# The down projection of an encoder trunk: 18 of 22 f-tiles by seven products, each product over all output pairs in turn

## The chip, the cores and the metric

The kernel runs on one core of one Trainium2 chip. The metric is the device time of one execution in microseconds (us), lower is better. The kernel before takes 1707.04 us, the median of 3 runs (1706.98 to 1707.08). Engines are named as in the profile: PE is TensorE (its matmuls), PEld its weight loads, DVE is VectorE, ACT is ScalarE, POOL is GpSimd, SP is SyncE, which here only issues DMAs.

## The reference, cut to what matters

One layer of a bidirectional encoder trunk: a convolution mixer and a gated linear recurrence side by side, a merge, and a gated feed-forward network (FFN) with a final norm. D_MODEL = 1024, SEQ = 1024, D_FF = 2816. Only the FFN bears on the change:

```python
def _conv_glu_ffn(h, w_up, dw_w, dw_b, w_down):
    up = jnp.einsum("bsd,df->bsf", h, w_up)
    gate, val = jnp.split(up, 2, axis=-1)
    gate = _dwconv_centred(gate, dw_w, dw_b)
    return jnp.einsum("bsf,fd->bsd", jax.nn.silu(gate) * val, w_down)
...
    x = x + _conv_glu_ffn(h2, ffn_w_up[layer], ...)
    return _rmsnorm(x, final_norm_w)
```

## The kernel before

Activations lie with the feature on the 128 partitions and the position along the free axis, in two halves of 512 positions. D_FF is 22 f-tiles of 128, D_MODEL is 8 output tiles of 128. Every float32 product is made of three matmuls on parts: a matrix is split into a high part (rounded by a cast on ACT) and a low part (the difference, on DVE, line 125, helper `split`), and `mm3` (lines 149 to 151) adds high-high, high-low and low-high in one PSUM bank. So each weight page and each activation page costs one ACT cast and one DVE subtraction before PE can use it, and the third matmul needs the low part of the weights.

The up projection (`ffn_job`, `pair_job`) makes two f-tiles' worth of work as a 2x2 block product by seven products in place of eight (Strassen's scheme as Winograd arranged it): P1, P2, P6, P7, P5, P4, P3 in that order, with sums of blocks on both sides. After each f-tile, `gated` makes silu(conv(gate)) * value, half by half: ACT L1708, two DVE operations L1710, ACT Silu L1718, DVE L1719 and L1720, and stores the half in the DRAM scratch `d_g`. For f-tiles that go into the seven-product part of the down projection, `g_sums` also makes the four sums of a pair of f-tiles and stores them in `d_gc`.

The down projection before has three parts. `std_down` takes the first 6 f-tiles plainly (8 output tiles x 2 halves x 6 f-tiles x 3 matmuls = 288 matmuls) and copies the results into the 16 result pages `xr`. `seven_down` takes the next 12 f-tiles in 2 rounds of 6, by seven products: a pair job for each of 4 pairs of output tiles (i, i+4), 3 k-steps a product (2 x 4 x 7 x 3 x 3 = 504 matmuls). Its results are added to `xr` on DVE (`take`, L1883; `f`, L1887), and in the last round POOL adds the residual `d_x2` to each page by an accumulating DMA (L1890). The sums of weight blocks that products 7, 5, 6 and 3 need are made by DVE adds inside the pair job, or for three of the eight jobs ahead of time (`down_sums`, L2036 to L2044), through the DRAM scratch `d_ws`. `last_jobs` takes the last 4 f-tiles plainly, adds them to `xr` (`final_evac`, L1954), and turns, normalises and stores the output.

What sets the order: PE's order is written out by hand (generators driven by `run_jobs` and `Stream`; `later(n, ...)` runs a chore n pieces of PE work later). The order of the other engines is made by a list scheduler, but instructions given to `pin` (`split(..., late=True)`, and the ACT steps of `gated`) keep their order in the program among themselves. Each engine, and SP's queue, then works strictly in its order. `std_job` splits its weights without `late`, the pair jobs with it. In SP's queue a DMA also waits for the landing of the one eight before it, as eight semaphores go round.

Page pools that matter: weight pages `wp` 4 (high and low of two items), `wr` 2 raw pages, activation pages `hx` 32 and `gx` 16, landing pages `ev` 3 and `tm` 4.

## Time and profile before

| | before |
|---|---|
| median of 3 runs | 1707.04 us |
| the profiled execution's own time | 1706.98 us |
| its span | 1705.0 us |
| mean granted PE clock | 0.999 |
| PE busy, share of the span | 99% |
| DVE, ACT busy | 74%, 49% |
| DMA, mean | 180 GB/s |

The span begins with the first and ends with the last instruction; 2.0 us of the execution lie around it. Busy PE is not PE at its peak, since matmuls overlap: what counts is the step from one matmul's start to the next one's. A matmul that starts late shows as idle time before it with what released it.

### The profile page before, as it was taken

Reading aid. Unit: us, or ns where it says so; the run is one execution under the profiler, and the core shown is the slowest. Engines: PE = TensorE matmul, PEld = TensorE weight load, DVE = VectorE, ACT = ScalarE, POOL = GpSimd, SP = SyncE. Lnnn points to the kernel's source line nnn. Section 1 sums busy time; section 2 is a strip of 40 time slices with the busy share of each in tenths; the row PEclk is TensorE's granted clock in tenths of the full one; section 3 lists DMA queues with packets and bytes.
Section 4 is the critical chain, followed back from the end, with each engine's and each line's share of the span. In section 5 each row is a group of like instructions: output and inputs, shape, how many; then the busy total and the mean of one; then the engine's idle time right before and its main releaser. Section 6 shows DMA issues by size and latency. Waiting matters only on the chain.

```text
span 1705.0 us, 30406 instructions
## 1 busy us (share of the span) xinstructions
PE 1688.6 (99%) x11719; PEld 1408.2 (83%) x11719; DVE 1269.3 (74%) x1938; ACT 827.3 (49%) x1562; POOL 245.9 (14%) x287
## 2 busy tenths in 40 slices
PE   9999999999999999999999999999999999999998
PEld 6788888888888888888888888888888888888787
DVE  5889899887678888888565467676777776657865
ACT  7454343335476777776432345444344434442334
POOL 1312222200001111111100003122222222000110
PEclk9999999999999999999999999999999999999999
DMA  7887887866573444436797455686777776773842
GB/s 240 284 213 186 191 196 172 205 187 206 165 236 100 139 129 134 129 116 221 241 294 243 128 167 176 153 171 143 172 164 178 164 183 149 237 260 102 212 98 99
DMA packets 332871, 306.17 MB, mean 180 GB/s; under 512 B 17454, under 2 KB 244918, under 8 KB 332726
## 3 DMA queue, kind: packets, MB, share of 16 engines
q1 hardware_dynamic: 285366, 265.42, 48.8%
q0 software_dynamic: 47360, 38.81, 15.4%
q8 instruction: 92, 1.51, 0.4%
q14 instruction: 53, 0.43, 0.1%
HBM read 201.40 MB, written 84.93 MB: 168 GB/s over the span
## 4 chain that ended last, share of the span: by engine, by line
PE 70%; ACT 1%; DVE 1%; DMA 0%; issue 0%; POOL 0%; POOLq 0%; ACTq 0%; DVEq 0%
PE mm L149 16%; PE mm L151 16%; PE mm L150 16%; PE sc L149 3%; PE sc L150 3%; PE sc L151 3%; PE ob L1433 2%; PE tr L149 2%; PE tr L150 2%; PE tr L151 2%; PE sc L1247 1%; PE sc L1333 1%; PE mm L1392 1%; PE sc L1392 1%; PE ob L1247 1%; PE tr L1382 0%
## 5 line engine op out<-in xcount | busy, mean ns | idle before, releaser
L149 PE MATMUL mm<-hx,wp 128*128 128x512 f32 x1068 | 425.7, 399 | 0.0
L151 PE MATMUL mm<-hx,wp 128*128 128x512 f32 x1068 | 417.0, 390 | 0.5 <-DVE wp L125 0.5
L150 PE MATMUL mm<-hx,wp 128*128 128x512 f32 x1068 | 416.2, 390 | 0.6 <-POOL hx L125 0.6
L125 ACT CAST wp<-wr 128x1024 fp32r<-128x1024 f32 (+2 forms) x146 | 146.9, 1006 | 224.3 <-PE mm L150 165.0
L151 PEld LDWEIGHTS mm<-hx,wp 128*128 128x128 f32 x1068 | 200.5, 188 | 44.6 <-DVE wp L125 1.6
L149 PEld LDWEIGHTS mm<-hx,wp 128*128 128x128 f32 x1068 | 200.6, 188 | 40.6 <-ACT wp L125 0.2
L150 PEld LDWEIGHTS mm<-hx,wp 128*128 128x128 f32 x1068 | 200.8, 188 | 39.9 <-POOL hx L125 1.0
L125 DVE TENSOR_TENSOR wp<-wr,wp 128x1024 fp32r<-128x1024 f32 (+2 forms) x144 | 169.5, 1177 | 39.8 <-ACT wp L125 39.4
L1065 DVE SCALAR_TENSOR_TENSOR acc<-gl,v_b,acc 128x1024 f32<-128x1024 f32 x120 | 153.5, 1280 | 1.7
L441 ACT COPY su<-mm 128x512 f32<-128x512 f32 x82 | 47.8, 583 | 84.4 <-PE mm L151 84.3
L1371 POOL DMA_DIRECT2D S<-D x64 | 36.1, 571 | 281.1 <-ACT jk L1438 125.3
L125 ACT CAST wq<-sw 128x1024 fp32r<-128x1024 f32 x41 | 43.2, 1054 | 61.3 <-PE mm L150 32.9
L1194 DVE TENSOR_TENSOR qF<-qF,tb 128x512 f32<-128x512 f32 x96 | 65.9, 686 | 9.5 <-ACT A L1228 8.9
L149 PE MATMUL tr<-hx,wp 128*128 128x512 f32 x180 | 70.1, 390 | 0.0
L151 PE MATMUL tr<-hx,wp 128*128 128x512 f32 x180 | 70.1, 389 | 0.0
L150 PE MATMUL tr<-hx,wp 128*128 128x512 f32 x180 | 70.0, 389 | 0.0
L1194 DVE TENSOR_TENSOR kG<-kG,tb 128x512 f32<-128x512 f32 x96 | 65.9, 687 | 4.0 <-ACT A L1228 2.2
L1710 DVE SCALAR_TENSOR_TENSOR tm<-gp,v_a,tm 128x512 f32<-128x512 f32 x88 | 66.0, 750 | 3.3 <-ACT tm L1708 1.3
L302 POOL DMA_DIRECT2D sw<-in_ffn_w_up_dram x38 | 49.8, 1502 | 116.0 <-DMA sw<-in_ffn_w_up_dram 72.4
L149 PE MATMUL sc<-hy,wq 128*128 128x512 f32 x164 | 63.9, 390 | 0.0
L151 PE MATMUL mm<-hy,wp 128*128 128x512 f32 x164 | 63.8, 389 | 0.0
L149 PE MATMUL mm<-hy,wp 128*128 128x512 f32 x164 | 63.8, 389 | 0.0
(377 smaller groups left out, 3721.9 us busy)
## 6 DMA issues: line engine op xcount, KB each, us to landing
wr<-in_w_in_dram SPq DMA_DIRECT2D x48, 512.0 KB, 5.6
wr<-in_ffn_w_up_dram SPq DMA_DIRECT2D x22, 512.0 KB, 5.6
sw<-in_w_in_dram SPq DMA_DIRECT2D x38, 256.0 KB, 3.1
d_g<-ft SPq DMA_DIRECT2D x38, 256.0 KB, 2.0
sw<-in_ffn_w_up_dram SPq DMA_DIRECT2D x38, 256.0 KB, 3.2
sw<-in_ffn_w_up_dram POOLq DMA_DIRECT2D x38, 256.0 KB, 6.7
wr<-sw POOLq DMA_DIRECT2D x32, 256.0 KB, 3.2
wr<-wr POOLq DMA_DIRECT2D x32, 256.0 KB, 3.3
```

What stands on the lines that cost most here:

```text
L125: parts = A.copy(hi, src), eng.tensor_tensor(lo, src, hi.bitcast(F32), op=ALU.subtract)
L149: T.matmul(acc, whi[:, k, :], ahi, start=first, stop=False, skip_group_check=again)
L150: T.matmul(acc, whi[:, k, :], alo, start=False, stop=False, skip_group_check=again)
L151: T.matmul(acc, wlo[:, k, :], ahi, start=False, stop=last, skip_group_check=again)
L302: G.dma_start(o, a, accum_op=ALU.add)
L441: A.copy(t, acc)
L1065: V.scalar_tensor_tensor(acc, g[:, k : k + S], tap(k), acc, op0=ALU.mult, op1=ALU.add)
L1194: return V.tensor_tensor(o, a, b, op=op)
L1247: T.matmul(b[g, o], A_t[:, at : at + 32], Q_t(at), start=True, stop=True)
L1371: G.dma_start(S_t[g : g + 32, :, g : g + 32], D_t[g : g + 32])
L1392: T.matmul(u[:, sl], kTs[d][:, sl], v[:, c, :], start=True, stop=True)
L1710: V.scalar_tensor_tensor(c, g[:, o + k : o + k + H], vec("fdw", k * NF + j), c, op0=ALU.mult, op1=ALU.add,)
```

## The change

The plain first part and the two rounds go. In their place 18 f-tiles (0 to 17) form one block product: even f-tiles are the upper half, odd ones the lower, 9 k-steps a product. The loop is turned round: a product is made for all four pairs of output tiles before the next product comes, so that its 9 activation pages are used four times. There are 28 items (product i, pair p) of 27 matmuls, in the order P1, P2, P6 for p = 0..3, then P7 and P4 for each p, then P5, P3 for p = 0..3. In all 756 matmuls stand in place of 792.

- Weights: an item loads 8 k-steps as one raw page of 128x1024; the ninth k-step of all four pairs is one page of 128x512 (`load_ninth`). Weight splits are made with `late`, so they are pinned.
- Sums of weight blocks now all go through `d_ws`: 36 tasks-worth of (p, k), each 4 loads of 64 KB, three in-place DVE adds (now pinned) and one store. 18 of them run during the up projection on `ev` pages, one an up job; the other 18 run early in the down projection as 10 tasks, in two `ws` pages of two k-steps.
- `g_sums` and its stores to `d_gc` run for nine pairs of f-tiles in place of six.
- PSUM: P1, P6, P5, P3 of a pair accumulate in one bank over the whole stage (`rows[p]`, four banks), P2, then P7 and P4 in `cols[p]`. P4 adds onto P7 in the same bank, after ACT has copied P7 out.
- Results: ACT copies P2, P7, P7+P4 and the last row into `xr`; DVE adds or subtracts the row bank for P2, P4 and P5 (12 operations where there were 56); the 16 accumulating DMAs of `d_x2` are spread over the stage.

The diff, cut:

```diff
-    FIRST, NS, SEVENS = 6, 3, 2
-    LAST0 = FIRST + 2 * NS * SEVENS
+    NS, LAST0 = 9, 18
+    d_ws = [dp.tile([P, 4, NS * P], F32, name=f"d_ws_{n}") for n in range(ND // 2)]
...
-            if hf and FIRST <= j < LAST0:
+            if hf and j < LAST0:
...
+    def down_sums(p, ks, page_of):
+        n = ks.stop - ks.start
+        t = page_of(n)
+        for q, (row, i) in enumerate(((0, p), (0, p + NK2), (1, p + NK2), (1, p))):
+            nc.sync.dma_start(t[:, q], down_rows(row, i)[:, ks])
+        def add():
+            for o, a in ((slice(0, 2), slice(1, 3)), (slice(2, 3), slice(0, 1)), (slice(3, 4), slice(2, 3))):
+                pin(V.tensor_tensor(t[:, o], t[:, o], t[:, a], op=ALU.add))
+            nc.sync.dma_start(d_ws[p]..., t)
+        later(DOWN_LATE, add)
...
-    for half in range(2):
-        for f in range(FIRST):
-            later(4, load_g(f, half))
-            s_ffn.fill(1)
+    for k in range(NS):
+        later(4, load_operand(1, k))
+        s_ffn.fill(1)
+    later(4, load_ninth(1))
     s_ffn.drain()
     advance_chores(1 << 10)
...
+    def down_job(g):
+        i, p = items[g]
+        def prep():
+            if g == 0:
+                for n in range(3):
+                    load_raw(n)
...
+            w = split(*pages, raws.pop(g), V, True)
+            load_raw(g + 3)
+            return w
+        def run(w):
+            if i == 1:
+                rows[p] = bank("mm" if p < 3 else "sc")
+            elif i in (2, 7):
+                cols[p] = bank(next(col_banks))
+            acc = cols[p] if i in (2, 7, 4) else rows[p]
+            fresh = i in (1, 2, 7)
+            for k in range(NS):
...
+            o, half = p + NK2 * (i in (4, 7, 5)), int(i in (7, 5, 3))
+            t = xr[o][half]
+            if i in (2, 4, 7, 3):
+                A.copy(t, acc)
+            if i in (2, 4, 5):
+                V.tensor_tensor(t, t, rows[p], op=ALU.add if i == 2 else ALU.subtract)
+            if i in (2, 4, 5, 3):
+                added(t, o, half)
...
+    for n, (p, ks) in enumerate(tasks):
+        later(3 + 2 * n, lambda p=p, ks=ks: down_sums(p, ks, down_page))
```

How the order moves, at three places. In the changed kernel's own numbering, lines 1654, 1656, 1664, 1665, 1666 and 1687 are the former 1708, 1710, 1718, 1719, 1720 and 1741; 126 is the former 125.

First, ACT where the up projection ends and the down projection begins. `gp` is the last f-tile's gate. Before, the rows at the end of `gated`, and the casts of weights for the first plain jobs (`wp_15359` is that of the first job):

```order
L1708 ACTIVATE tm_15152<-gp_12008,v_c,v_a 128x512
L125 CAST wp_15359<-wr_15357 128x768
L1718 ACTIVATE tm_15152<-tm_15152 128x512
...
L125 CAST wp_15377<-wr_15375 128x768
L125 CAST hx_15301<-tm_15257 128x512
L125 CAST hx_15307<-tm_15271 128x512
L1708 ACTIVATE tm_15311<-gp_12009,v_c,v_a 128x512
L1718 ACTIVATE tm_15311<-tm_15311 128x512
L1708 ACTIVATE tm_15319<-gp_12009,v_c,v_a 128x512
L125 CAST wp_15434<-wr_15432 128x768
L1718 ACTIVATE tm_15319<-tm_15319 128x512
```

Now, the same place (`wp_15543` is the high part of item 0's weights, `wp_15607` that of item 2):

```order
L126 CAST hx_15477<-ev_15432 128x512
L1654 ACTIVATE tm_15489<-gp_12010,v_c,v_a 128x512
L1664 ACTIVATE tm_15489<-tm_15489 128x512
L1654 ACTIVATE tm_15497<-gp_12010,v_c,v_a 128x512
L1664 ACTIVATE tm_15497<-tm_15497 128x512
L126 CAST wp_15543<-wr_15537 128x1024
L126 CAST wp_15549<-wr_15539 128x1024
L126 CAST hx_15589<-tm_15535 128x512
L126 CAST hx_15601<-tm_15562 128x512
L126 CAST wp_15607<-wr_15541 128x1024
```

The first weights of the down projection stood one f-tile ahead of the last gating; they now stand behind all of it, and the same holds on DVE for the low part.

Second, DVE some 24 us into the changed down projection, where nothing like it stood before. `ws` are the pages of the stored sums, `wq_15747` and `wq_15820` the low parts of the weights of items 4 and 5 (P2, pairs 0 and 1), `gx_15814` that of the ninth weight page of P2:

```order
L1784 TENSOR_TENSOR ws_15649<-ws_15649 128x512
L1784 TENSOR_TENSOR ws_15649<-ws_15649 128x256 x2
L126 TENSOR_TENSOR wq_15747<-sr_15553,wq_15746 128x1024
L126 TENSOR_TENSOR gx_15760<-tm_15701,gx_15759 128x512
L1784 TENSOR_TENSOR ws_15682<-ws_15682 128x256
L1784 TENSOR_TENSOR ws_15682<-ws_15682 128x128 x2
L126 TENSOR_TENSOR gx_15790<-tm_15732,gx_15789 128x512
L1784 TENSOR_TENSOR ws_15709<-ws_15709 128x512
L1784 TENSOR_TENSOR ws_15709<-ws_15709 128x256 x2
L126 TENSOR_TENSOR gx_15814<-tm_15763,gx_15813 128x512
L126 TENSOR_TENSOR wq_15820<-sr_15611,wq_15819 128x1024
```

The adds of the fourth, fifth and sixth task of stored sums stand ahead of splits that PE waits for.

Third, DVE where item 8 (P6, pair 0) begins. `xr_15516` is the result page of item 7, `wq_15994` and `wq_16052` the weights of items 8 and 9, `ws_15832` the tenth and last task, `gx_15921` to `hx_16030` the activation pages of P6 from its fourth on, `hx_16045` its ninth weight page:

```order
L126 TENSOR_TENSOR wq_15994<-sr_15823,wq_15993 128x1024
L1924 TENSOR_TENSOR xr_15516<-xr_15516,sc_15752 128x512
L1784 TENSOR_TENSOR ws_15832<-ws_15832 128x256
L126 TENSOR_TENSOR wq_16052<-sr_15889,wq_16051 128x1024
L1784 TENSOR_TENSOR ws_15832<-ws_15832 128x128 x2
L126 TENSOR_TENSOR gx_15921<-ev_15873,gx_15920 128x512
...
L126 TENSOR_TENSOR hx_16030<-ev_15985,hx_16029 128x512
L126 TENSOR_TENSOR hx_16045<-ev_16010,hx_16044 128x512
```

Six of the nine pages that P6 reads are split only behind the evacuation of the item before it and behind the last sums.

## The prediction

> **What bounds the kernel now.** I read the head of the page and the busy time, the list of what PE waited for, PE's timeline at the start of the down projection, and then the busy time of stretches.

> ```profile
> span 1705.0 us, 30406 instructions
> PE 1688.6 (99%) x11719; PEld 1408.2 (83%) x11719; DVE 1269.3 (74%) x1938; ACT 827.3 (49%) x1562; POOL 245.9 (14%) x287
> PE sc L149 <- ACT su L441: 0.6, 1, 0.6
> PE mm L151 <- DVE wp L125: 0.5, 1, 0.5
> ```

> PE is busy throughout, and its waits are few and short. So a removed matmul is worth one step of PE, and any new wait of PE is lost in full. The timeline's columns are start, duration, engine, line, what is written and read:

> ```profile
> 1463.47 0.39 PE L151 MATMUL mm<-hy,wp 128*128 128x512 f32 x1
> 1463.69 0.39 PE L149 MATMUL mm<-hx,wp 128*128 128x512 f32 x1
> ...
> 1464.15 0.39 PE L151 MATMUL mm<-hx,wp 128*128 128x512 f32 x1
> ...
> 1465.96 0.39 PE L150 MATMUL mm<-hx,wp 128*128 128x512 f32 x1
> ...
> 1644.65 0.39 PE L149 MATMUL mm<-hx,hx 128*128 128x512 f32 x1
> ```

> The first row is the last matmul of the up projection, the second the first of the down projection, with no gap. From 1463.69 to 1465.96 there are ten steps: 2.27 / 10 = 0.227 us a step, although one matmul shows 0.39. The first matmul of `last_jobs` starts at 1644.65, so the part that is rewritten takes 1644.65 - 1463.69 = 180.96 us for its 792 matmuls.

> The profiled execution took 1706.98 us (span 1705.0 and 2.0 around it), 0.06 below the median of 1707.04. All sums below are made against 1706.98.

> **What the change removes: 9.4 us.** 756 matmuls at 0.227 take 171.6 us if none waits: 180.96 - 171.6 = 9.4. Of this 36 x 0.227 = 8.2 are the removed matmuls, and the other 1.2 are short gaps of before, which go with the loops that had them:

> ```profile
> 1590.00:1600.00 10.00, 9.21 (x40) 7.02 (x39) 9.74 (x17) 2.00 (x4) 1.73 (x2) 1.00 0.89 258
> ```

> (window, length, then busy us of PE, PEld, DVE, ACT, POOL, granted clock, DMA share, GB/s). PE stood still for 0.8 us here beside a nearly full DVE. DVE also loses 44 of 56 evacuations, but DVE isn't what sets the end.

> **What it adds, first: the handover, 9.6 us.** The order of ACT shows item 0's weight cast behind the second Silu of the last f-tile, and DVE's order its low part behind the last L1720. PE has nothing else to do. Before, the same chain ran under running matmuls:

> ```profile
> 1464.22 0.68 DVE L1741 TENSOR_TENSOR gp<-mm,rs 128x512 f32<-128x512 f32 x1
> 1464.82 0.95 DVE L125 TENSOR_TENSOR wp<-wr,wp 128x768 fp32r<-128x768 f32 x1
> 1465.68 1.29 DVE L125 TENSOR_TENSOR hx<-tm,hx 128x512 fp32r<-128x512 f32 x2
> 1466.89 1.53 DVE L1710 SCALAR_TENSOR_TENSOR tm<-gp,v_a,tm 128x512 f32<-128x512 f32 x2
> 1469.12 0.69 DVE L1719 TENSOR_TENSOR tm<-tm,rs 128x512 f32<-128x512 f32 x1 [0.70 <-ACT tm L1718]
> 1469.85 0.69 DVE L1720 TENSOR_TENSOR ft<-ft,tm 128x512 f32<-128x512 f32 x1
> 1470.46 1.53 DVE L1710 SCALAR_TENSOR_TENSOR tm<-gp,v_a,tm 128x512 f32<-128x512 f32 x2
> 1468.45 0.63 ACT L1718 ACTIVATE tm<-tm 128x512 f32<-128x512 f32 x1 [2.13 <-DVE tm L1710]
> L125 ACT CAST wp<-wr 128x1024 fp32r<-128x1024 f32 x127 | 133.4, 1050 | 204.4 <-PE mm L150 146.3 <-PE tr L150 32.8 <-DMA wr<-wr 15.5
> L125 DVE TENSOR_TENSOR wp<-wr,wp 128x1024 fp32r<-128x1024 f32 x127 | 155.7, 1226 | 24.9 <-ACT wp L125 24.6
> ```

> On the clock of before: `gp` starts at 1464.22, 0.60 to the next; one split of 0.6 in place of the three shown: the first L1710 pair starts at 1465.4. From there 2.23 to L1719 (1466.89 to 1469.12), 0.73 to L1720, 0.61 to the second pair: 1469.0. Its Silu starts 1.56 after it (1466.89 to 1468.45) and takes 0.63: 1471.2. The cast takes 1.05: PE may start at 1472.2. DVE is free at 1469.0 + 2.23 + 0.73 + 0.69 = 1472.6, and the low part takes 1.23: the third matmul starts at 1473.8, where 1464.15 was undisturbed. That is 9.65 us; 9 to 10.5 with a queue's delay. This term alone eats the gain.

> **Second: the stored sums beside the first items, 12 us.** An item lasts 27 x 0.227 = 6.13 us. DVE now adds ten tasks, in its fixed order between splits that PE needs, and they pass through two pages:

> ```profile
> L2042 DVE TENSOR_TENSOR sr<-sr,sr x6: 551/558/560, 1484.1 to 1497.8; 128x384 f32<-128x384 f32 x6
> DMA to landing us min/median/max: 3.9/5.6/7.4
> tm<-d_g SPq DMA_DIRECT2D x21, 256.0 KB, 3.5
> d_g<-ft SPq DMA_DIRECT2D x4, 256.0 KB, 2.0
> 1486.79 0.39 SPq L2036 DMA_DIRECT2D sr<-in_ffn_w_down_dram  x1
> ```

> A page's round trip: four issues of about 0.4 (1.6), landing about 3.5 behind the last (2.5 to 5, between the rows of 256 KB and 384 KB), adds 1.4, store about 3 (2 to 4; 256 KB take 2.0 when little else runs): 9.5 us for two tasks, before any queueing on DVE or SP. Counting from the start of item 0: the low part of item 3 waits for a `wp` page, that is for PE at about 11.4; the second task's adds, behind it, end at 15.0. The fourth's then end a round trip later, at 24.6, and item 4's low part, behind them, at 25.8; PE needs it at 24.75: a wait of 1.05. The sixth's end another round trip and 1.9 of adds and splits ahead of them later, at 36.0, and the ninth page of P2, behind them, is split at 36.7, where PE needs it at 31.2 (24.5, the 1.05 and 24 steps of the item): 5.5. Item 5 behind that costs about 0.5. At item 8 the evacuation of item 7, the last adds and the next low part (1.23) stand ahead of P6's fourth page: 2.0; and P6's ninth page, which needs the last store, a load and a split: 2.8. Together about 12; with the short landings 6, with the long ones 18. I take 12, since the landing is the row nearest in size.

> **Third: P4 onto P7, 3.2 us.** P4 starts in the bank that ACT must first copy:

> ```profile
> L441 ACT COPY su<-mm 128x512 f32<-128x512 f32 x82 | 47.8, 583 | 84.4 <-PE mm L151 84.3
> ```

> PE has no other work between P7 and P4 of a pair. The last matmul ends 0.39 - 0.227 = 0.16 after its step, the copy takes 0.58: about 0.8 with the signal, four times. The wait of 0.6 quoted at the start is of this kind, so 2.4 to 4.

> **Fourth: the entry to the last jobs, 2.4 us.** Their first weight casts now stand on ACT behind the copy of the last row bank, which waits for the last matmul:

> ```profile
> 1648.49 0.62 ACT L125 CAST gx<-wr 128x512 fp32r<-128x512 f32 x1 [12.76 <-DMA wr<-in_ffn_w_down_dram]
> ```

> 0.16 + copy 0.58 + two casts of 0.62, and part of a low part (0.69): 2.4, between 1.5 and 3.

> **Fifth: the clock, 2.7 us.** PE has never stood still for long in the trace of before, except at its end:

> ```profile
> 1697.22 0.41 PE L1970 MATMUL sc<-ident,xr 128*128 128x128 f32 x2 [0.39 <-DVE xr L1954]
> 1698.00:1700.00 2.00, 0.00 (x0) 0.00 (x0) 1.02 (x5) 0.68 (x5) 0.70 (x1) 1.00 0.00 0
> 1700.00:1702.00 2.00, 0.00 (x0) 0.00 (x0) 0.68 (x2) 0.79 (x2) 0.00 (x0) 0.54 0.45 186
> ```

> The granted clock is still 1.00 two us behind the last matmul and 0.54 after 1700. Waits of 8 us and 5.5 us are longer than that, so PE comes back at about half clock. How fast it recovers the trace can't show. Between at once (0) and 3 us lost each, I take as long at half clock as it took to fall, 2.7 us: 1.35 lost, twice.

> [...]

> **Added, at nothing: the up projection.** 18 early tasks and three more pairs of `g_sums` add about 1 us of DVE adds to a job, 256 KB of loads and a store.

> ```profile
> 1250.00:1300.00 50.00, 50.00 (x222) 41.44 (x221) 37.91 (x52) 19.80 (x28) 11.34 (x10) 1.00 0.83 191
> ```

> PE is full while DVE has 12 of 50 us free and DMA a sixth. PE's work hides it: 0, and 2 at most if it comes late.

> **Sum.** -9.4 + 9.6 + 12 + 3.2 + 2.4 + 2.7 = +20.5: 1706.98 + 20.5 = 1727. Low ends: -9.4 + 9 + 6 + 2.4 + 1.5 + 0 = +9.5, 1716.5. High ends: -9.4 + 10.5 + 18 + 4 + 3 + 6 + 2 = +34, 1741.

> **The rivals.** *The stored sums hide.* If loads and stores land at their shortest and DVE gets to each add at once, the second term falls to 0 to 4 and the clock's to half: +7 to +11 less a little at the other ends, 1710 to 1717. For it: DVE is busy only 11.4 of 20 us at this place before.

> ```profile
> 1463.00:1483.00 20.00, 20.00 (x90) 16.56 (x89) 11.40 (x17) 8.26 (x14) 0.00 (x0) 1.00 0.80 242
> ```

> Against: a fixed order with two pages, and a round trip of over 9 us.

> *DMA is the bound.* The first 65 us move about 18 x 512 KB of sums, 10 weight pages of 512 KB and 18 or more pages of 256 KB, some 20 MB or 308 GB/s, an estimate.

> ```profile
> 1490.00:1500.00 10.00, 10.00 (x46) 8.29 (x45) 7.79 (x14) 3.47 (x6) 0.00 (x0) 1.00 1.05 345
> ```

> 345 GB/s was had only at full share. If landings double to 7 us, each of four round trips grows by 3.5 to 5: 14 to 20 more, and some in the up projection: 1741 to 1760.

> *The other side: the handover is short.* If item 0 gets its weights before the last gating, because its cast stands free when PE ends, the first term falls to about 3 and, with hidden sums and no loss of clock, -9.4 + 3 + 2.4 + 1.5 = -2.5: 1704.5; with the copies hidden too, 1700. It decides at stalls of 9.4 us together. Against it: the casts are pinned behind the Silu, and the rows give the chain 8 us with nothing to shorten it.

> That the change doesn't do what it says is left out: the order has the 36 matmuls fewer.

> **Chances.** Forecast 1717 to 1741: 0.66. Hidden sums, 1710 to 1717: 0.14. DMA, 1741 to 1760: 0.11. Other side: 0.09, of which 0.05 faster and 0.04 within 0.2% (3.4 us, about what a measurement of this kernel can tell from no change). Slower: 0.91. The range should hold 8 in 10: the forecast's with a part of both neighbours, 1713 to 1743.

> **What would show it.** Right: some 8 us of idle PE near 1464 that ends with ACT's cast of `wp`, then 1.5 for the low part on DVE; PE waits for `gx` and `wq` low parts in the fifth, sixth and ninth items, with SP waiting for stores of `ws`; four waits of about 0.8 on ACT's copy; one of about 2.4 on a cast at the last jobs; a granted clock near 0.5 behind the two long waits. Wrong: no wait at the handover (first term falls), waits in the first ten items under 3 us together (second term), or waits during the up projection (its cost of nothing).

## The result, and the profile after

The changed kernel takes 1736.62 us, the median of 4 runs (1734.41 to 1738.51), against 1707.06 (4 runs): 1.0172 times as long, 95% interval 1.0155 to 1.019. The forecast was 1727 in a range of 1713 to 1743. The profiled execution took 1734.41.

The head of the page, and then, from the list of what PE waited for, the lines of the down projection and of the entry to the last jobs (engine, line, releaser: us in total, times, longest):

```profile
span 1732.6 us, 30626 instructions
PE 1690.9 (98%) x11683; PEld 1405.2 (81%) x11683; DVE 1266.4 (73%) x1962; ACT 834.8 (48%) x1566; POOL 243.9 (14%) x287
PE mm L1909 <- ACT wp L126: 8.0, 1, 8.0
PE mm L1909 <- DVE gx L126: 4.9, 1, 4.9
PE tr L1909 <- DVE gx L126: 2.8, 1, 2.8
PE tr L1909 <- DVE wq L126: 2.0, 1, 2.0
PE mm L150 <- ACT hx L126: 1.7, 1, 1.7
PE mm L1909 <- ACT hx L126: 1.4, 1, 1.4
PE ob L1909 <- ACT xr L1922: 1.4, 2, 0.7
PE tr L1909 <- ACT xr L1922: 1.3, 2, 0.7
PE tr L1909 <- ACT gx L126: 1.3, 1, 1.3
```

There are 36 matmuls fewer (11719 to 11683), and none of these waits was there before. L1909 is the matmul of the new down projection. PE's timeline puts them in order of time; the last columns are the count, and in brackets the wait before the first of them:

```profile
1472.36 1.22 PE L1909 MATMUL mm<-hx,wp 128*128 128x512 f32 x2 [7.99 <-ACT wp L126]
1502.45 3.96 PE L1909 MATMUL tr<-hx,wq 128*128 128x512 f32 x16 [2.02 <-DVE wq L126]
1509.05 0.73 PE L1909 MATMUL tr<-gx,gx 128*128 128x512 f32 x2 [1.28 <-ACT gx L126]
1512.63 0.80 PE L1909 MATMUL tr<-gx,gx 128*128 128x512 f32 x1 [2.85 <-DVE gx L126]
1541.35 1.22 PE L1909 MATMUL mm<-gx,wq 128*128 128x512 f32 x2 [4.85 <-DVE gx L126]
1548.29 1.23 PE L1909 MATMUL mm<-hx,hx 128*128 128x512 f32 x3 [1.43 <-ACT hx L126]
```

These are the handover, item 4, the ninth page of P2 (twice), P6's fourth page and P6's ninth page: the places that the prediction named. The two matmuls at 1472.36 show 1.22 us, where 16 at 1502.45 take 3.96, so some steps are slow as well. The stretches of two us (length, busy us of PE, PEld, DVE, ACT, POOL, granted clock, DMA share, GB/s) show why:

```profile
1466.00:1468.00 2.00, 0.00 (x0) 0.00 (x0) 1.27 (x3) 0.82 (x2) 0.00 (x0) 0.81 0.68 240
1474.00:1476.00 2.00, 1.99 (x5) 1.61 (x6) 2.00 (x3) 0.29 (x1) 0.00 (x0) 0.50 0.98 277
1478.00:1480.00 2.00, 2.00 (x10) 1.64 (x9) 0.00 (x0) 0.00 (x0) 0.00 (x0) 1.00 0.97 332
1516.00:1518.00 2.00, 2.00 (x6) 1.52 (x6) 1.48 (x2) 0.16 (x1) 0.81 (x1) 0.50 1.09 352
1542.00:1544.00 2.00, 2.00 (x6) 1.60 (x5) 1.47 (x3) 0.62 (x1) 0.00 (x0) 0.50 1.15 311
```

At a granted clock of 0.50, five or six matmuls fit in 2 us in place of ten. That happens behind three of the waits, not two.

The spans of the profiled executions differ by 27.6 us: 1732.6 - 1705.0. The steps between PE's matmuls add up to it:

| part | forecast | in the trace |
|---|---|---|
| matmuls and old gaps removed | -9.4 | -9.1 |
| wait at the handover | +9.6 | +8.4 |
| waits at the stored sums | +12 | +12.4 |
| P4 onto P7 | +3.2 | +2.7 |
| entry to the last jobs | +2.4 | +1.7 |
| steps over 0.227 us beside the waits (clock, first steps behind a wait) | +2.7 | +10.2 |
| ahead of and behind the rewritten part | 0 | +1.3 |

The rows add up to 20.5 and 27.6. The medians differ by 29.6: the profiled execution was the fastest of the four, and what the others waited for longer isn't on record. The handover's 8.4 are 7.99 and 0.43, the second for the low part of the weights; the waits at the stored sums are 2.02 + 1.28 + 2.85 + 4.85 + 1.43. The row on slow steps is what the steps of the down projection exceed 0.227 by in all, 35.5 us, less the waits of 25.3 in the four rows above it.

### The profile page after: what moved, and what is told of

It is laid out like the page before. It is cut to its first block, busy times and chain, and to the rows that moved or that the text cites. A ratio compares the mean times of both kernels' runs of the same rounds, so it can differ in the third digit from the quotient of the medians.

```text
span 1732.6 us, 30626 instructions
## 1 busy us (share of the span) xinstructions
PE 1690.9 (98%) x11683; PEld 1405.2 (81%) x11683; DVE 1266.4 (73%) x1962; ACT 834.8 (48%) x1566; POOL 243.9 (14%) x287
## 4 chain that ended last, share of the span: by engine, by line
PE 66%; DMA 2%; ACT 2%; DVE 1%; SPq 1%; issue 1%; POOL 0%; POOLq 0%; ACTq 0%; DVEq 0%
PE mm L150 14%; PE mm L152 13%; PE mm L151 13%; PE mm L1909 4%; PE sc L150 2%; PE sc L151 2%; PE sc L152 2%; PE ob L1388 2%; PE ob L1909 1%; PE tr L1909 1%; PE tr L150 1%; PE tr L152 1%; PE tr L151 1%; PE sc L1909 1%; PE sc L1202 1%; DMA d_ws<-ws 1%
## 5 line engine op out<-in xcount | busy, mean ns | idle before, releaser
L150 PE MATMUL mm<-hx,wp 128*128 128x512 f32 x920 | 368.2, 400 | 0.0
L151 PE MATMUL mm<-hx,wp 128*128 128x512 f32 x920 | 358.8, 390 | 0.6 <-POOL hx L126 0.6
L152 PE MATMUL mm<-hx,wp 128*128 128x512 f32 x920 | 359.4, 391 | 0.0
L126 ACT CAST wp<-wr 128x1024 fp32r<-128x1024 f32 (+1 forms) x154 | 156.8, 1019 | 219.0 <-PE mm L151 148.3
L126 DVE TENSOR_TENSOR wp<-wr,wp 128x1024 fp32r<-128x1024 f32 (+1 forms) x152 | 181.2, 1193 | 53.0 <-ACT wp L126 48.8
L152 PEld LDWEIGHTS mm<-hx,wp 128*128 128x128 f32 x920 | 172.7, 188 | 37.8 <-DVE wp L126 0.6
L150 PEld LDWEIGHTS mm<-hx,wp 128*128 128x128 f32 x920 | 172.8, 188 | 34.8 <-ACT wp L126 0.2
L151 PEld LDWEIGHTS mm<-hx,wp 128*128 128x128 f32 x920 | 173.1, 188 | 34.2 <-POOL hx L126 1.0
L151 PE MATMUL mm<-hy,wp 128*128 128x512 f32 x164 | 63.9, 390 | 0.0
L150 PE MATMUL tr<-hx,wp 128*128 128x512 f32 x164 | 63.9, 390 | 0.0
L150 PE MATMUL sc<-hy,wq 128*128 128x512 f32 x164 | 63.9, 390 | 0.0
L152 PE MATMUL tr<-hx,wp 128*128 128x512 f32 x164 | 63.8, 389 | 0.0
L150 PE MATMUL mm<-hy,wp 128*128 128x512 f32 x164 | 63.8, 389 | 0.0
L152 PE MATMUL sc<-hy,wq 128*128 128x512 f32 x164 | 63.8, 389 | 0.0
## 6 DMA issues: line engine op xcount, KB each, us to landing
sw<-in_w_in_dram SPq DMA_DIRECT2D x38, 256.0 KB, 3.1
sw<-in_ffn_w_up_dram SPq DMA_DIRECT2D x38, 256.0 KB, 4.6
sw<-in_ffn_w_up_dram POOLq DMA_DIRECT2D x38, 256.0 KB, 6.4
d_gc<-ft SPq DMA_DIRECT2D x36, 256.0 KB, 3.3
d_g<-ft SPq DMA_DIRECT2D x35, 256.0 KB, 3.4
wr<-sw POOLq DMA_DIRECT2D x32, 256.0 KB, 3.5
```

The source lines that it names most:

```text
L126: parts = A.copy(hi, src), eng.tensor_tensor(lo, src, hi.bitcast(F32), op=ALU.subtract)
L150: T.matmul(acc, whi[:, k, :], ahi, start=first, stop=False, skip_group_check=again)
L151: T.matmul(acc, whi[:, k, :], alo, start=False, stop=False, skip_group_check=again)
L152: T.matmul(acc, wlo[:, k, :], ahi, start=False, stop=last, skip_group_check=again)
```

## The experiments

All times stand beside runs of the kernel before on the same chip; its medians lie within 0.4 us of each other. The changed kernel was not run again beside them. Its four runs spread by 4 us, and single waits differ from one execution to the next: P6's fourth page waits 4.9 us in it, 5.0 in e4 and 6.8 in e7, and the edits of both come later in the program. So differences of a few us between medians are rough. The first batch undoes one part each.

**e1, the first splits not pinned.** In `down_job`:

```diff
-            w = split(*pages, raws.pop(g), V, True)
+            w = split(*pages, raws.pop(g), V, g > 1)
```

> The weight splits of items 0 and 1 are not pinned, so that they can stand ahead of the last gating; nothing else changes. Theory (the handover is a term of its own): the waits of 8.0 and 0.4 us behind the up projection go, and with them some 2 us of slow steps behind them: about 10 us less than the changed kernel, 1726. Rival (SP's queue sets the pace): the loads of the next items stand in SP's order behind the stores of the last f-tile and do not move; then PE waits at items 2 to 5 instead, and the gain is below 5 us, 1732 or more.

It takes 1734.79 (1734.58 to 1736.0), 1.0161 times before (1.0146 to 1.0176): not to be told from the changed kernel. The handover's wait is gone, and PE waits in item 3 for as long. PE's, DVE's and SP's timelines of e1:

```profile
1491.55 7.83 PE L1909 MATMUL sc<-hx,wp 128*128 128x512 f32 x22 [7.87 <-DVE wp L126]
```

```profile
1488.15 1.61 DVE L1784 TENSOR_TENSOR ws<-ws 128x512 f32<-128x512 f32 x3 [10.33 <-DMA ws<-in_ffn_w_down_dram]
1489.68 0.68 DVE L126 TENSOR_TENSOR hx<-tm,hx 128x512 fp32r<-128x512 f32 x1
1490.28 1.22 DVE L126 TENSOR_TENSOR wp<-wr,wp 128x1024 fp32r<-128x1024 f32 x1
```

```profile
1476.11 0.32 SPq L1668 DMA_DIRECT2D d_g<-ft  x1
...
1480.33 6.97 SPq L1780 DMA_DIRECT2D ws<-in_ffn_w_down_dram  x8
```

The first adds of sums wait 10.3 us for a load, and item 3's low part (1490.28) stands behind them. The load was issued only after the store of the last f-tile (L1668) in SP's queue. So the chain of sums begins at the last gating, whatever PE does, and the 8 us come back. The rival held.

**e2, all sums in the up projection.**

```diff
-DOWN_EARLY, DOWN_AT, DOWN_STEP, DOWN_LATE = 18, 16, 14, 6
+DOWN_EARLY, DOWN_AT, DOWN_STEP, DOWN_LATE = 36, 16, 8, 6
```

> All 36 sums are made in the up projection, one every 8 pieces in place of every 14. Theory (the stored sums beside the first items cost PE the waits): the waits at item 4, at the ninth page of P2 and at P6 (2.0, 1.3 and 2.8, 4.9, 1.4) go with the slow steps behind them (about 5): some 17 us less than the changed kernel, 1719 to 1721, and no new waits in the up projection. Rival (the up projection hasn't the room): waits of PE before 1464 us, the gain below 8 us, 1729 or more.

1725.03 (1723.46 to 1726.86), 11.6 less than the changed kernel, between the two theories. The waits at items 4 and 8 and at the ninth pages are gone, but the list of PE's waits has two others:

```profile
PE mm L1909 <- ACT wp L126: 12.1, 1, 12.1
...
PE mm L150 <- ACT su L399: 2.0, 4, 0.8
```

The handover grew from 8.0 to 12.1, and in the up projection PE's steps exceed 0.227 by 4.9 us in all, where those of the changed kernel do by 0.04. There is room for 18 sums, not for 36 at this pace.

**e3, the late adds left out** (the ten tasks keep their loads and stores):

```diff
-                pin(V.tensor_tensor(t[:, o], t[:, o], t[:, a], op=ALU.add))
+                if page_of is sums_page:
+                    pin(V.tensor_tensor(t[:, o], t[:, o], t[:, a], op=ALU.add))
```

> The DVE adds of the ten late tasks are left out (d_ws then holds blocks without their sums); their loads and stores stay. Theory (DVE's fixed order carries the wait: splits stand behind adds that wait for a load): the waits at item 4, at the ninth page of P2 and at P6's fourth page fall from 2.0, 4.1 and 4.9 to under 1 each, 10 us and some 5 of slow steps: 1720 to 1724. Rival (DMA or SP's queue is late by itself): the waits stay above half, 1730 or more.

1734.79 (1731.87 to 1736.02): the theory fell. PE's timeline, then the waits of SP's queue:

```profile
1512.74 1.65 PE L1910 MATMUL tr<-gx,gx 128*128 128x512 f32 x3 [6.88 <-ACT gx L126]
1540.59 0.50 PE L1910 MATMUL mm<-hx,wq 128*128 128x512 f32 x1 [2.99 <-ACT hx L126]
```

```profile
SPq L1780 <- DMA d_ws<-ws: 10.6, 6, 3.0
```

```profile
1502.36 4.20 SPq L1780 DMA_DIRECT2D ws<-in_ffn_w_down_dram  x8
1506.66 0.41 SPq L1877 DMA_DIRECT2D wr<-in_ffn_w_down_dram  x1
1507.11 2.00 SPq L1835 DMA_DIRECT2D tm<-in_ffn_w_down_dram  x4
```

The waits behind the handover still sum to 12 us. Item 4's is gone, but P2's ninth page (L1835) is issued at 1507, behind loads of sums (L1780) that wait for a page's store to land; its cast and PE come after that. So DVE's adds aren't needed for the loss.

**e4, P7 of two pairs and then P4 of both.**

```diff
-    items += [(i, p) for p in range(NK2) for i in (7, 4)]
+    items += [(i, p + n) for p in (0, 2) for i in (7, 4) for n in range(2)]
```

> P7 of two pairs, then P4 of both, in place of P7 and P4 of each pair. Theory (PE waits for the copy of the bank that it adds onto): the four waits of 0.68 go with their slower first steps, 4 x 0.8 = 3.3 us less than the changed kernel, 1733. Rival (another wait, for the operands of P4 or for weights, ends where these did): four waits remain at the same places, no change.

1732.41 (1731.37 to 1732.83), 4.2 less. The four waits on ACT's copy are gone from the list, so the theory held. The price isn't settled by it: the profiled executions differ by 2.1 (1734.41 to 1732.3), since in e4 the waits at the stored sums are 1.4 us longer.

The second batch asks who carries the sums' wait, and tests the two smaller terms.

**e5, the ten tasks on POOL's queue.** Loads and stores of the late tasks, in `down_sums`:

```diff
-            nc.sync.dma_start(t[:, q], down_rows(row, i)[:, ks])
+            (nc.sync if page_of is sums_page else G).dma_start(t[:, q], down_rows(row, i)[:, ks])
...
-            nc.sync.dma_start(d_ws[p].rearrange("p q (k e) -> p q k e", e=P)[:, :, ks], t)
+            (nc.sync if page_of is sums_page else G).dma_start(d_ws[p].rearrange("p q (k e) -> p q k e", e=P)[:, :, ks], t)
```

> The loads and stores of the ten late tasks are issued on POOL's queue in place of SP's; the adds and all else stay. Theory now (SP's queue in its order carries the wait: loads of weights and operands stand behind loads of sums that wait for a page's store): the four waits in the first ten items, 12.4 us in the changed kernel, fall below 6, with the slow steps behind them: 1727 or less. Rival (the DMA engines themselves are full in 1510 to 1560, or DVE's adds still wait for their loads): the waits stay above 10 us, 1733 or more.

1748.43 (1747.58 to 1748.8), the slowest of all. PE's longest wait, the waits of DVE, and two stretches:

```profile
1509.37 5.94 PE L1909 MATMUL tr<-hx,wq 128*128 128x512 f32 x14 [9.22 <-DVE wq L126]
```

```profile
DVE ws L1784 <- DMA ws<-in_ffn_w_down_dram: 37.0, 6, 8.1
```

```profile
1490.00:1500.00 10.00, 10.00 (x45) 8.08 (x43) 3.69 (x7) 3.28 (x6) 4.39 (x7) 1.00 0.68 230
1500.00:1510.00 10.00, 0.78 (x3) 0.54 (x3) 3.45 (x7) 0.00 (x0) 5.60 (x9) 0.72 0.56 194
```

Now DVE carries the wait: its adds wait 37 us for loads, and item 4's low part stands behind them. POOL works in order as well, so a page's loads stand behind the other page's store, which waits for its adds; and an issue takes a median of 0.73 us there, against 0.47 on SP's queue in the changed kernel. In the ten us in which PE stands still, the DMA engines are busy for 0.56 of the time: their capacity is not the bound there, which speaks against the rival of the prediction that made it so. In the changed kernel the share was higher, 0.90 from 1500 to 1515 and 0.99 from 1515 to 1545, so e5 doesn't exclude that full DMA engines had a part in the waits there.

**e6, PE kept busy at the handover.** On top of e2, in `run` of item 0:

```diff
+            if g == 0:
+                idle = bank("tr")
+                for _ in range(48):
+                    T.matmul(idle, gs[1, 0][0][:, :P], gs[1, 0][0], start=True, stop=True)
```

> All sums in the up projection as before it in e2 (1725.0), and 48 matmuls more on PE into a bank that nobody reads, ahead of item 0, to fill most of the wait of 12 us at the handover; their results are not used. Theory (the slow steps behind a long wait are the clock, which falls when PE stands still): the granted clock stays at 1.00 there, the first steps of item 0 take 0.23 in place of 0.43 to 0.59, 2.5 to 3 us less than e2: 1722.3. Rival (the steps are slow because parts of weights or pages come late): no change against e2.

1722.11 (1721.14 to 1724.35), 2.9 less than e2, as the theory said, but not for its reason. In the two profiled executions the last matmul of the up projection starts at 1465.45 in e6 and at 1468.89 in e2, so 3.4 us are won ahead of the handover, 2.7 of them by shorter waits and fewer slow steps in the up projection. From there to the third matmul of item 0 both take 14.1 us. The stretches of e6 behind the handover:

```profile
1476.00:1478.00 2.00, 0.86 (x5) 0.40 (x4) 1.27 (x3) 1.76 (x3) 0.00 (x0) 1.00 1.02 338
1478.00:1480.00 2.00, 1.08 (x4) 0.60 (x5) 2.00 (x3) 1.79 (x3) 0.00 (x0) 1.00 0.88 303
1482.00:1484.00 2.00, 2.00 (x7) 1.57 (x6) 0.00 (x0) 0.00 (x0) 0.00 (x0) 0.53 0.82 256
```

The clock is at 1.00 when item 0 starts (e2: 0.50), and falls in the middle of it, with PE at work, behind two remaining waits of 1.1 and 0.9. So the theory fell in that the clock wasn't held. The run does show that the slow steps are the clock's, since they are slow at 0.53 while nothing is waited for. And it gives a part of their price: behind the third matmul of item 0 the slow steps make 2.5 us in e2 and 1.7 in e6, 0.8 less.

**e7, the last jobs' entry earlier.**

```diff
-            todo.append((6 * per + 1 + int(2.5 * (2 * (f - LAST0) + half)), f, -1 - half))
+            todo.append((6 * per - 6 + int(2.5 * (2 * (f - LAST0) + half)), f, -1 - half))
...
+    st.fill(6 * per + 12 - st.count)
+    for prep, _ in last[:2]:
+        prep()
```

> The first two weight splits of the last jobs and the loads of their activation pages are issued some pieces earlier, so that their casts stand ahead of the copy of the last row bank. Theory: the wait of 1.7 us at the first last job goes with the slower first steps, 2.3 us less than the changed kernel: 1734.3. Rival (another operand of the first last job is late too): the gain is below 1 us.

1732.93 (1732.45 to 1736.02), 3.7 less. The wait of 1.7 is gone from the list; a wait of 0.5 on an evacuation stands near it. More than forecast, but within the spread of 4 us of the changed kernel's runs; the profiled execution is even 1.6 longer than that of the changed kernel (1736.02 to 1734.41), with the longer wait at P6's fourth page in it. So the wait's cause is shown, and its price is not.

**e8, the edits of e1, e4, e5 and e7 in one kernel.**

> Early splits (e1), P7 and P4 apart (e4), POOL's queue (e5) and the early entry (e7) in one kernel. Theory (with the late sums off SP's queue, the handover's wait isn't given back): the terms add, 1736.6 less 10 less 3.3 less 2.3 and less what e5 gives: 1707 to 1713. Rival (the start of the sums' chain at the last gating sets the pace whatever PE does): the handover's 10 us come back as waits at items 3 to 8, 1718 or more.

1737.42 (1734.87 to 1739.3): by its number the rival. PE waits 10.4 us at item 4 behind DVE, and 7.6 at P6's ninth page. But e8 holds the edit of e5, which is 11.8 us slower than the changed kernel by itself. Against e5 the three other edits gain 11.0 of the 15.6 that they were priced at. The handover's 8.4 us are gone, and the waits behind it at weights and pages grow from 24.0 us in e5 to 28.7, so about half of that gain is given back to the chain of sums.

The third batch takes the chain away.

**e9, no late tasks at all** (pairs 2 and 3 read plain blocks where they would read sums):

```diff
+        if p >= 2:
+            return down_rows(int(i != 6), p)
...
-    for n, (p, ks) in enumerate(tasks):
-        later(3 + 2 * n, lambda p=p, ks=ks: down_sums(p, ks, down_page))
```

> The ten late tasks are left out whole (loads, adds, stores); pairs 2 and 3 read plain weight blocks in place of their sums, at the same sizes. Theory (the ten tasks cost what the waits show): no waits of PE in the first twelve items behind the handover, 12.4 us and about 5 of slow steps less than the changed kernel: 1719. Rival (operands and weights are late without the tasks too): waits of over 4 us stay there, 1724 or more.

1715.44 (1714.8 to 1716.51), 21.2 less than the changed kernel; of the profiled executions 19.0 (1734.41 to 1715.36). Between the handover and the copies of P7 no wait is left. The lines of the down projection and the entry to the last jobs:

```profile
PE mm L1911 <- ACT wp L126: 8.2, 1, 8.2
PE mm L150 <- ACT hx L126: 1.7, 1, 1.7
PE tr L1911 <- ACT xr L1924: 1.4, 2, 0.7
PE ob L1911 <- ACT xr L1924: 1.4, 2, 0.7
PE mm L1911 <- DVE wp L126: 0.4, 1, 0.4
```

So the ten tasks, with their DMA traffic, cost 12.4 us of waits and about 6.2 of slow steps behind them; the handover waits 0.2 longer here, and the rewritten part is 18.5 us shorter in the trace.

**e10, the edits of e1 and e2.**

> e1 and e2 together: no sums beside the first items, and the splits of items 0 and 1 not pinned. Theory (the handover is a cost of its own once no chain behind it starts at the last gating): its wait of 12 us and 3 us of slow steps in e2 go: 1710 to 1712. Rival (the wait moves again, since the loads of items 2 and 3 stand behind the last gating's stores in SP's order): 1718 or more.

1715.17 (1712.4 to 1719.06), 9.9 less than e2, between the two theories. With no sums beside the items, the handover's gain stays, for the most part: waits of 0.5, 1.7, 0.7 and 0.5 are left among items 0 to 4. The up projection loses 6.2 us in this execution.

**e11, the edits of e10, e4 and e7**, with the sums from piece 4, one every 7.8 pieces.

> e10, e4 and e7 in one kernel, with the sums in the up projection begun a little earlier (one every 7.8 pieces from piece 4). Theory: e10 less 3.3 less 2.3: 1704 to 1706, the 36 matmuls less the waits of the up projection. Rival (SP or the up projection gives back more): 1708 or more.

1706.87 (1705.35 to 1710.47, 11 runs) against 1707.21: 1.0 times before (0.9991 to 1.0009), no difference. It keeps the 36 matmuls less, and pays in the up projection:

```profile
PE mm L150 <- ACT su L399: 2.6, 4, 1.1
```

With shorter waits and the slower steps beside them the up projection loses 5.6 us. Behind it two longer waits are left, 0.9 in item 2 and 1.3 in the last jobs. At one of the places in the up projection the trace shows ACT's copy behind a cast of weights that had waited 5.9 us for its DMA.

**e12, 27 sums in the up projection, the others spread.** As e11, but with

```diff
+DOWN_EARLY, DOWN_AT, DOWN_STEP, DOWN_LATE = 27, 6, 10.5, 6
...
-        later(3 + 2 * n, lambda p=p, ks=ks: down_sums(p, ks, down_page))
+        later(3 + 6 * n, lambda p=p, ks=ks: down_sums(p, ks, down_page))
```

> As e11, but 27 sums in the up projection (one every 10.5 pieces) and the other 9 as five tasks beside the items, one every 6 pieces in place of every 2. Theory (the two-page round trip of the sums is what costs, and it fits where a page has 12 pieces, some 16 us, before it is wanted again; the up projection pays for density of sums): PE waits of the up projection fall from 4.4 us (e11) to 2 or less, and the first twelve items wait no more than 2 us: 1702 to 1705. Rival (any sums beside the first items hold up SP's queue): waits of 4 us or more there, 1707 or more.

1711.74 (1711.19 to 1712.9), 1.0027 times before (1.0017 to 1.0037). By its number the rival held; the trace says something narrower. The up projection has no wait at all, and the items have three waits, PE's and DVE's timelines:

```profile
1477.00 0.73 PE L1909 MATMUL mm<-hx,wp 128*128 128x512 f32 x2 [0.77 <-ACT wp L126]
1478.68 5.30 PE L1909 MATMUL mm<-hx,wp 128*128 128x512 f32 x22 [0.95 <-DVE wp L126]
1492.68 7.68 PE L1909 MATMUL sc<-hx,wp 128*128 128x512 f32 x22 [7.56 <-DVE wp L126]
```

```profile
1489.27 1.61 DVE L1784 TENSOR_TENSOR ws<-ws 128x512 f32<-128x512 f32 x3 [10.04 <-DMA ws<-in_ffn_w_down_dram]
```

It is e1's wait again: the first task's adds stand ahead of item 3's low part, and its load comes after the last gating. The four tasks behind it cost PE nothing, so the two pages suffice for five tasks at one every 6 pieces; e12 has fewer late tasks and wider spacing at once, and doesn't tell the two apart. Without this one wait and the slow steps behind it (7.6 and about 2.7) the kernel would take 1701 to 1702, an estimate that holds only if nothing comes back elsewhere, as it did in e1; a first task that starts later was not tried.

## Why the prediction was right, and what it mis-sized

**Removed matmuls.** 9.4 was forecast and 9.1 is in the trace. A step of 0.227 holds, to about 0.01, where nothing is waited for and the granted clock is 1.00.

**The handover.** 9.6 against 8.4 of waits. The prediction counted to the third matmul, and counted so the delay is 9.4, since slow steps between the first and the third make the rest. Its chain runs as worked out: PE starts with ACT's cast, and the third matmul 1.65 us later with the low part. What the prediction didn't see is that this term couldn't be had back by itself (e1): it and the next one are one chain, anchored at the last gating. As a sum they were rightly added, since both stand in the same order.

**The stored sums.** 12 against 12.4 in the trace; the places were right and their sizes mixed: 2.0 in place of 1.05 at item 4, 4.1 in place of 5.5 at P2's ninth page, 4.9 in place of 2.0 at P6's fourth, 1.4 in place of 2.8 at its ninth, and nothing in place of 0.5 at item 5. That the sum met so closely is luck: errors from -1.4 to +2.9 cancel. (The working has two slips of 0.2 us. If the third matmul is the one that needs the low part, PE needs it at 24.97 in item 4, not at 24.75; and 24.5, 1.05 and 24 steps make 31.0, not 31.2.) The cause was only half right. The prediction put the wait on splits behind adds in DVE's order; e3 shows nearly the same loss with no adds, through SP's order, and e5, with the tasks on POOL's queue, a larger one, through POOL's order and DVE's. What they have in common is the round trip of the two pages, asked for early and densely. That the ten tasks cost the loss is shown (e9); that the round trip does it, and not the load on the DMA engines, is argued: the loads of sums landed in a median of 3.2 us (128 KB) and 4.9 (64 KB), near the forecast's 3.5 and short of the 7 of the DMA rival, but the DMA share was 0.9 and more. e12 shows that five tasks at one in 6 pieces cost nothing, but for the first.

**P4 onto P7** and **the entry** held: 3.2 against 2.7 of waits, and 2.4 against 1.7, or 3.3 and 1.9 with the 0.16 that a last matmul ends behind its step, which the prediction had counted in. e4 and e7 show what each waits for; their medians are too rough for a price. **The up projection at nothing** held for the 18 sums and, by e12, for 27; e2 and e11 show the end of that cover at 36.

**The clock** is the term that was mis-sized: 2.7 was forecast, and slow steps make 10.2, of which some 8.3 lie behind three waits, 2.7 at the handover, 3.3 at P2's ninth page and 2.3 at P6's fourth. Two things were wrong in it. The prediction counted two long waits, since P6's fourth page was put at 2.0 us. And the slow stretch was taken as long as the fall, 2.7 us, where it lasts longer: from 1472.4 to 1477.5, from 1512.6 to 1518.5 and from 1541.4 to 1545.8, 5.1, 5.8 and 4.4 us of steps mostly of 0.43. The last section shows what PE did until the clock was back. The remaining 2 us are the steps beside the other waits: 0.16 ahead of each, which the prediction had counted in P4 and the entry, and a first step of about 0.34 in place of 0.227 behind it, which it left out.

## What to carry to other kernels

Before 36 matmuls of 0.227 us are bought, look at what the new order puts ahead of the first of them: a term that hangs on an in-order queue comes back elsewhere when only its first victim is helped, so price and move the whole chain, from where it is anchored. The two scratch pages here had a round trip of some 10 us (in the changed kernel one page is stored at 1498.6, 1509.0 and 1519.1). They were free, but for the first task, where five tasks wanted a page again after some 15 us (12 pieces), and dear where ten wanted it after 5 (4 pieces); moving their DMAs to POOL's queue made the kernel 12 us slower. In the changed kernel the waits of 7.99 and 4.85 us on a PE that was full cost their length and 2.7 and 2.3 us more in slow steps, and two shorter ones close together, 1.28 and 2.85, cost 3.3 more.

## What the runs showed of the hardware

In the changed kernel's trace the clock is at 0.50 three times before the last jobs: from 1467.26 to 1477.50, from 1511.63 to 1518.46 and from 1538.94 to 1545.77, that is for 10.24, 6.83 and 6.83 us. Between them it is at 1.00 for 34.13 and 20.48 us. The five lengths are 3, 2, 2, 10 and 6 times 3.41. Here are stretches of that length, laid both ways from the first fall (columns as in the first such table):

```profile
1463.85:1467.26 3.41, 0.51 (x3) 0.09 (x1) 3.10 (x5) 0.87 (x3) 0.00 (x0) 1.00 0.56 177
1470.67:1474.09 3.42, 1.30 (x3) 0.59 (x3) 2.69 (x5) 3.35 (x5) 0.00 (x0) 0.50 0.38 137
1474.09:1477.50 3.41, 3.41 (x8) 2.74 (x9) 2.20 (x3) 0.20 (x1) 0.00 (x0) 0.50 0.92 232
1497.98:1501.39 3.41, 2.44 (x11) 1.69 (x9) 3.31 (x8) 0.62 (x1) 0.00 (x0) 1.00 0.69 214
1501.39:1504.81 3.42, 2.36 (x10) 1.96 (x11) 1.60 (x2) 0.62 (x1) 0.00 (x0) 1.00 0.98 305
1508.22:1511.63 3.41, 0.73 (x2) 0.30 (x2) 1.20 (x3) 1.56 (x2) 0.00 (x0) 1.00 0.93 265
1511.63:1515.05 3.42, 2.42 (x6) 1.90 (x7) 2.40 (x4) 1.46 (x3) 0.00 (x0) 0.50 0.88 268
1515.05:1518.46 3.41, 3.41 (x10) 2.64 (x9) 2.59 (x4) 1.11 (x2) 0.86 (x1) 0.50 1.07 340
1518.46:1521.87 3.41, 3.41 (x17) 2.80 (x16) 1.14 (x3) 0.00 (x0) 0.00 (x0) 1.00 1.08 314
1535.53:1538.94 3.41, 0.97 (x5) 0.47 (x3) 0.38 (x2) 0.28 (x1) 0.86 (x1) 1.00 0.98 265
1538.94:1542.35 3.41, 1.00 (x2) 0.83 (x3) 3.38 (x7) 1.24 (x2) 0.00 (x0) 0.50 0.95 286
1542.35:1545.77 3.42, 3.42 (x9) 2.64 (x8) 1.45 (x3) 0.89 (x2) 0.00 (x0) 0.50 1.01 305
```

Item 4's wait lies across 1501.39, so PE is still busy for 2.44 and 2.36 us of the two stretches, and the clock stays. From 1508.22 PE is busy for 0.73 us only, and the clock falls at the stretch's end, before the wait of 2.85 is over. Ahead of the other two falls PE is busy for 0.51 and 0.97 us. After each fall PE comes back within a stretch at 0.50, in which it is busy for 1.30, 2.42 and 1.00 us; the next stretch is still at 0.50, with PE busy throughout, and behind that one the clock is at 1.00. So PE works at half clock for 5.1, 5.8 and 4.4 us, where the prediction took 2.7. Whether the busy time of such a stretch decides, or the length of a wait, these three falls don't show; no run moved a wait on purpose.
